# Four PSUM banks for more of the projections, four z tiles computed beside the mLSTM heads, and loads of the branch stages issued from GpSimd

## The chip, the cores and the metric

The kernel runs on one core of a Trainium2 chip. TensorE (PE) multiplies matrices into PSUM, VectorE (DVE), ScalarE (ACT) and GpSimd (POOL) work on tiles, and SyncE (SP) mostly issues transfers. Each engine runs its instructions in a fixed order that a scheduler sets when the program is built; an instruction that waits holds up everything behind it on its engine. A transfer issued by SP, ACT or POOL is one instruction in that engine's order. The metric is the time of one execution in microseconds (us), lower is better.

## What is computed

One layer of a hybrid backbone over 1024 latent tokens of width 1024, with a prefix of 256 context tokens. Two recurrent mixers read the same modulated input `u`, an mLSTM with 8 heads and a gated linear attention (GLA) with 4 heads, both in two directions. Their outputs are normalized, gated and merged, and a convolutional GLU follows. Cut to what the change touches:

```python
mod = jax.nn.silu(c) @ w_mod[l] + b_mod[l]            # 6 x 1024, the modulation vector
p = u @ w_in + b_in                                   # q, k, v, o, z and the gates of both mixers
q_m, k_m, v_m, o_m, g_m, q_g, k_g, v_g, z_g, r_g, gate_a, gate_b = jnp.split(p, cuts, axis=-1)
y_m = (head_norm(h_m, mlstm_norm_g, True) * jax.nn.sigmoid(o_m)) @ w_branch_mlstm
y_g = (head_norm(h_g, gla_norm_g, False) * jax.nn.silu(z_g)) @ w_branch_gla
mix = (jax.nn.sigmoid(gate_a) * y_m + jax.nn.sigmoid(gate_b) * y_g) @ w_out
```

## The kernel before

**Matmuls.** All float32 products are made of three matmuls in a reduced format (high x high, high x low, low x high; lines L283, L284, L285 of `mm3`), eight blocks deep: a group of 24 matmuls fills one PSUM bank of 128x512. Weights are loaded by SP in pieces, split by an ACT copy (L252) and a subtraction on DVE or POOL (L253). PSUM has eight banks in four tags of two each: `pj`, `pa`, `po`, `pt`. A group that is the third of its tag has to wait until the first one has been copied out.

**GLA stage.** For each of four heads: `gla_qk` and `gla_v` project (tag `pj`), `log_gates` (L423 to L435) makes the decays of the heads, `gla_scan` runs seven levels, each an ACT copy (L612), two PSUM tiles of products (L618, tag `pa`), and on DVE a masked copy (L619) and updates (L624, L626, L628). Level by level L618 needs the `qq` of L626. L596 is the diagonal part ahead of the levels. The scheduler places the projections of the next head and a gate tile between the levels.

**mLSTM stage.** For each of eight heads: `ml_proj_qk` of the next head (tag `pj`, with the short convolution in L727 to L747 on ACT and DVE), at every second head `ml_proj_v`, the end of the head before (`late`, L844 to L847), then `ml_scan`: POOL issues three broadcast loads per direction (L760, L762, L764), ACT takes exponentials of them in place (L765 and L769), PE multiplies (L777, L786, L796, L816, L817). Then `fill` computes gate tiles as filler: `gate_tile` makes one 128x1024 tile of the gates, two groups of tag `pj`, copied out by ACT (L537, tile `gt`) and stored to DRAM (L538) as `thb` or `tha`. Sixteen such tiles are spread over both stages.

**Branch stages.** `gated` with O_ZG computes the z tiles, takes silu of them and multiplies the GLA outputs (`hr`, loaded from DRAM). The GLA branch (L945 to L959) multiplies by its weights, 16 groups, and by the gate (`thb`, L953), and stores `ya`. In the same loop `mod_sum` forms the second part of the modulation vector, 4096 values in eight pieces: four loads of 512 KB each (L906) into two buffers in turn, eight accumulating steps on DVE (L908), after POOL has cleared the accumulator (L901) and a piece of `b_mod` has been loaded into it. `mod_row` adds the 128 partitions up with two matmuls (L913), copies the row (L914) and stores it (`md_d`, L915). There is one accumulator. SP issues all those loads and stores. Then `gated` with O_OM makes the o stage, and the mLSTM branch (L980 to L998) merges.

## Time and profile before

| | before |
|---|---|
| time, median of 3 runs | 2317.84 us (2316.33 to 2319.12) |
| the profiled execution | 2320.08 us, span 2318.3 us |
| mean granted TensorE clock | 0.991 |
| packets of transfers | 246.56 MB, mean 106 GB/s |
| stages, about | GLA 137 to 500 us, mLSTM 500 to 1100, z 1100 to 1195, GLA branch 1195 to 1285 and its row vectors to 1345, o and mLSTM branch to 1484 |

A view of waits has one row for an engine, a line and what it waited for: microseconds in total, how often, the longest. A view of windows cuts the span in stretches and gives for each engine busy time and number of instructions, the granted clock as a fraction of full speed, and the traffic. A timeline has start, duration, engine, line, output and input tiles, and in brackets the idle time before the instruction and what ended it. Times are of the profiled execution.

### The profile page before, as it was taken

How to read it: one execution, taken by the hardware profiler on the slowest of the kernel's cores; microseconds unless marked ns; L12 is line 12 of the kernel's file. 1: busy time of each engine (PE TensorE's matmuls, PEld its weight loads, DVE VectorE, ACT ScalarE, POOL GpSimd, SP SyncE). 2: the span in 40 equal slices, each digit the busy share in tenths (PEclk: the TensorE clock that was granted, in tenths of full speed). 3: DMA queues.
4: the chain of work that ended last, by engine and by line, in shares of the span. 5: the costliest groups of instructions: out<-in, count | busy, mean ns of one | idle time of the engine just before them, and what ended most of it. 6: DMA issues, size and time to landing. Idle time of an engine off the chain costs nothing.

```text
span 2318.3 us, 30341 instructions
## 1 busy us (share of the span) xinstructions
PE 2241.0 (97%) x11641; PEld 1881.1 (81%) x11641; DVE 1323.9 (57%) x2511; ACT 728.3 (31%) x1239; POOL 253.9 (11%) x254
## 2 busy tenths in 40 slices
PE   8989999998999999999999999999999999999998
PEld 4979898987888888897876788787788888888886
DVE  6485737376563665656345543477856556554257
ACT  3563323224323331322432133312433333333110
POOL 1010101011110111101110032101210000000100
PEclk9999999999999999999999999999999999999999
DMA  8231121104332433324346645524411222225721
GB/s 284 67 118 51 59 69 44 60 26 106 98 100 57 116 97 97 104 64 119 100 145 219 209 130 159 179 81 143 130 37 55 62 66 77 75 92 188 219 77 73
DMA packets 187747, 246.56 MB, mean 106 GB/s; under 512 B 16257, under 2 KB 129537, under 8 KB 187601
## 3 DMA queue, kind: packets, MB, share of 16 engines
q1 hardware_dynamic: 164673, 179.16, 24.5%
q0 software_dynamic: 12416, 44.21, 7.2%
q10 hardware_dynamic: 10512, 21.24, 2.5%
q8 instruction: 92, 1.51, 0.3%
q14 instruction: 54, 0.44, 0.1%
HBM read 186.57 MB, written 49.60 MB: 102 GB/s over the span
## 4 chain that ended last, share of the span: by engine, by line
PE 76%; DMA 8%; issue 6%; DVE 6%; ACT 2%; POOL 1%; SPq 0%; DVEq 0%; POOLq 0%; ACTq 0%
PE pj L283 15%; PE pj L284 15%; PE pj L285 15%; DMA qq<-re 2%; DMA u<-in_w_mod_dram 2%; PE pa L618 2%; PE po L284 2%; PE po L283 2%; PE po L285 2%; PE pa L285 2%; PE pa L284 2%; PE pa L283 2%; DMA s<-rr 1%; PE pt L796 1%; PE po L816 1%
## 5 line engine op out<-in xcount | busy, mean ns | idle before, releaser
L283 PE MATMUL pj<-u,whi 128*128 128x512 f32 (+1 forms) x816 | 315.8, 387 | 17.0 <-DVE s L743 5.7
L253 DVE TENSOR_TENSOR wlo<-raw,whi 128x512 fp32r<-128x512 f32 x302 | 218.0, 726 | 167.2 <-ACT whi L252 163.2
L284 PE MATMUL pj<-u,whi 128*128 128x512 f32 (+1 forms) x816 | 313.0, 384 | 0.0
L285 PE MATMUL pj<-u,wlo 128*128 128x512 f32 (+1 forms) x816 | 312.8, 384 | 0.0
L252 ACT ACTIVATE whi<-raw 128x512 fp32r<-128x512 f32 x302 | 188.8, 629 | 385.2 <-PE pj L285 155.2
L285 PE MATMUL pj<-s,wlo 128*128 128x512 f32 x784 | 305.7, 390 | 2.0 <-DVE wlo L253 2.0
L283 PE MATMUL pj<-s,whi 128*128 128x512 f32 x784 | 305.4, 390 | 0.4 <-ACT val L1118 0.4
L284 PE MATMUL pj<-s,whi 128*128 128x512 f32 x744 | 290.4, 390 | 3.0 <-POOL s L1086 3.0
L1142 DVE SCALAR_TENSOR_TENSOR acc<-g,colF,acc 128x945 f32<-128x945 f32 (+2 forms) x168 | 206.4, 1229 | 139.8 <-ACT acc L1133 137.8
L283 PEld LDWEIGHTS pj<-u,whi 128*128 128x128 f32 x816 | 155.2, 190 | 47.9 <-ACT s L769 11.1
L283 PE MATMUL pj<-whi,u 128*128 128x256 f32 x640 | 181.7, 284 | 0.0
L285 PE MATMUL pj<-whi,u 128*128 128x256 f32 x640 | 181.4, 283 | 0.0
L284 PE MATMUL pj<-wlo,u 128*128 128x256 f32 x640 | 181.4, 283 | 0.0
L285 PEld LDWEIGHTS pj<-u,wlo 128*128 128x128 f32 x816 | 155.2, 190 | 26.5
L284 PEld LDWEIGHTS pj<-u,whi 128*128 128x128 f32 x816 | 155.3, 190 | 25.7
L285 PEld LDWEIGHTS pj<-s,wlo 128*128 128x128 f32 x784 | 147.2, 188 | 33.2 <-DVE wlo L253 2.7
L283 PEld LDWEIGHTS pj<-s,whi 128*128 128x128 f32 x784 | 147.2, 188 | 32.0 <-ACT val L1118 0.8
L284 PEld LDWEIGHTS pj<-s,whi 128*128 128x128 f32 x744 | 139.7, 188 | 34.4 <-POOL s L1086 4.3
L283 PEld LDWEIGHTS pj<-whi,u 128*128 128x128 f32 x640 | 122.8, 192 | 0.5
L284 PEld LDWEIGHTS pj<-wlo,u 128*128 128x128 f32 x640 | 122.8, 192 | 0.0
L285 PEld LDWEIGHTS pj<-whi,u 128*128 128x128 f32 x640 | 122.8, 192 | 0.0
L727 DVE SCALAR_TENSOR_TENSOR s<-pj,colB,s 128x511 f32<-128x511 f32 (+2 forms) x96 | 57.5, 613 | 85.1 <-ACT s L732 84.2
(496 smaller groups left out, 4044.1 us busy)
## 6 DMA issues: line engine op xcount, KB each, us to landing
u<-in_w_mod_dram SPq DMA_DIRECT2D x48, 512.0 KB
raw<-in_w_in_dram SPq DMA_DIRECT2D x96, 256.0 KB
raw<-in_w_up_dram SPq DMA_DIRECT2D x176, 128.0 KB
raw<-in_w_in_dram SPq DMA_DIRECT2D x96, 128.0 KB
raw<-in_w_down_dram SPq DMA_DIRECT2D x44, 256.0 KB
s<-rmask POOLq DMA_DIRECT2D x16, 512.0 KB, 4.9
s<-rr POOLq DMA_DIRECT2D x16, 512.0 KB, 7.9
qq<-re POOLq DMA_DIRECT2D x16, 512.0 KB, 6.5
```

What stands on the lines that cost most here:

```text
L252: A.activation(hi, src, AF.Copy)
L253: eng.tensor_tensor(lo, src, hi.bitcast(F32), op=ALU.subtract)
L283: T.matmul(p, lh, rh, start=k == 0, stop=False)
L284: T.matmul(p, lh, rl, start=False, stop=False)
L285: T.matmul(p, ll, rh, start=False, stop=k == nk - 1)
L618: T.matmul(p[:, c, :], kc[:, o:o + P], pairs(qq, 1, hs, o, 64 // hs), start=True, stop=True)
L727: V.scalar_tensor_tensor(y[:, o:o + src.shape[1]], src, t, y[:, o:o + src.shape[1]], op0=ALU.mult, op1=ALU.add)
L796: T.matmul(p[:, i, :], kt[d][:, c, :], v[:, c, :], start=True, stop=True)
L816: T.matmul(p[:, i, :], dt_[d][:, c, :], v[:, c, :], start=True, stop=False)
L1142: V.scalar_tensor_tensor(av, g[:, r0 + dy:r1 + dy, c0 + dx:c1 + dx], convw(3 * ky + kx, f), av, op0=ALU.mult, op1=ALU.add)
```

## The change

Five edits. (1) The projections of GLA (`gla_qk`, `gla_v`, and the gate tiles beside GLA heads) take their banks from `pj` and `po` in turn instead of `pj` alone. (2) `ml_proj_qk` and the gate tiles beside mLSTM heads take theirs from `pj` and `pa` in turn; `ml_proj_v` stays with `pj`. (3) Tiles 0 to 3 of z are computed (without their tanh) as gate tiles and stored to DRAM (`thz`); the heads of the mLSTM have 2, 2, 2, 1, 1, 2, 2, 3 fills instead of 2, 2, 1, 1, 1, 1, 2, 2, and one more fill stands behind them. `gated` loads these four tiles instead of computing them. (4) In `gated`, the two branches and `mod_sum`, the loads `hr`, `thz`, `thb`, `tha`, `ya` and `w_mod` are issued by POOL instead of SP; the two `thb` loads of a tile are issued ahead of `mod_sum`. SP keeps the weights, `b_mod` and the stores. (5) The modulation sums have two accumulators (tiles 17 and 19), and the matmuls of a row come one tile later in the program.

```diff
@@ -529,10 +529,10 @@
             parts.append((hi, lo))
         return lambda k, c, n: tuple(t[:, k % 4, c:c + n] for t in parts[k // 4])
 
-    def gate_tile(dst, off, cb0, j):
+    def gate_tile(dst, off, cb0, j, tags=("pj", "pj")):
         w = wtile(w_in, off + j * P)
         for b in range(2):
-            p = proj(w, 0, b)
+            p = proj(w, 0, b, tags[b])
             t = sc.tile([P, 512], F32, tag="gt", name=nm("gt"), bufs=2)
             A.activation(t[:], p[:], AF.Identity, scale=0.5, bias=cB(cb0 + j))
             A.dma_start(dst[j][:, b * 512:b * 512 + 512], t[:])
@@ -542,10 +542,10 @@
         q = slot(0, [P, SEQ])
         k = slot(1, [P, L])
         for b in range(2):
-            p = proj(w, 0, b)
+            p = proj(w, 0, b, ("pj", "po")[b])
             A.activation(q[:, b * 512:b * 512 + 512], p[:], AF.Identity, scale=QS, bias=cB(c_qg + h))
         for b in range(3):
-            p = proj(w, P, b)
+            p = proj(w, P, b, ("pj", "po")[b % 2])
             A.activation(k[:, b * 512:b * 512 + BW[b]], p[:, 0:BW[b]], AF.Identity, bias=cB(c_kg + h))
         return q, k
 
@@ -554,7 +554,7 @@
         w = wload([(w_in, O_VG + h * 256, 256, 0)], eng=V)
         vs = [slot(2 + 2 * (h % 2) + i, [P, 5, 256]) for i in range(2)]
         for t0 in range(0, 10, 2):
-            p = pt("pj", [P, 2, 256])
+            p = pt(("pj", "po")[t0 // 2 % 2], [P, 2, 256])
             for i in range(2):
                 mm3(p[:, i, :], u_tok(t0 + i), lambda k: w(k, 0, 256))
             if t0 < 8:
@@ -728,7 +728,7 @@
                                        op0=ALU.mult, op1=ALU.add)
             for b in range(2 + i):
                 m, o = BW[b], b * 512
-                p = proj(w, i * P, b)
+                p = proj(w, i * P, b, ("pj", "pa")[(i + b) % 2])
                 A.activation(y[:, o:o + m], p[:, 0:m], AF.Identity, scale=t1, bias=bs)
                 tap(o + 1, p[:, 0:m - 1], t0)
                 tap(o, p[:, 1:m], t2)
@@ -853,11 +853,14 @@
         while rest:
             rest.pop()()
 
-    gates = [(thb_d, O_GB, c_gb, j) for j in range(8)] + [(tha_d, O_GA, c_ga, j) for j in range(8)]
-
-    def fill(n):
+    NZ = 4
+    thz_d = [drt(f"thz{j}", [P, SEQ]) for j in range(NZ)]
+    gates = [(thb_d, O_GB, c_gb, j) for j in range(8)] + [(tha_d, O_GA, c_ga, j) for j in range(8)] + \
+        [(thz_d, O_ZG, c_zg, j) for j in range(NZ)]
+
+    def fill(n, tags=("pj", "pj")):
         for _ in range(n):
-            gate_tile(*gates.pop(0))
+            gate_tile(*gates.pop(0), tags)
 
     for h in range(GH):
         q, k = gla_qk(h) if h else (q0, k0)
@@ -866,10 +869,10 @@
         if h == 0:
             for i in range(1, GH):
                 log_gates(i)
-            fill(1)
+            fill(1, ("pj", "po"))
         rest.append(gla_scan(h, q, k, v))
         if h:
-            fill(1)
+            fill(1, ("pj", "po"))
     v2 = ml_proj_v(0)
     rr_d, re_d, decb, (ta, twk, tem) = ml_gates()
     qk = ml_proj_qk(0)
@@ -881,7 +884,7 @@
         late()
         rest.append(ml_scan(h, *qk, v2[h % 2]))
         qk = nxt
-        fill(2 if h < 2 or h > 5 else 1)
+        fill((2, 2, 2, 1, 1, 2, 2, 3)[h], ("pj", "pa"))
     late()
     while gates:
         fill(1)
@@ -897,13 +900,13 @@
         return tags[seq[0] % 3]
 
     def mod_sum(b):
-        acc = ubt(19, [P, 512])
+        acc = ubt((17, 19)[b % 2], [P, 512])
         G.memset(acc[:], 0.0)
         c0 = 2048 + b * 512
         SY.dma_start(acc[0:1, :], I["b_mod"][c0:c0 + 512].unsqueeze(0))
         for k2 in range(0, KD, 2):
             raw = ubt((16, 18)[k2 // 2 % 2], [P, 2, 512])
-            SY.dma_start(raw[:], I["w_mod"][k2 * P:(k2 + 2) * P, c0:c0 + 512].rearrange("(k p) c -> p k c", p=P))
+            G.dma_start(raw[:], I["w_mod"][k2 * P:(k2 + 2) * P, c0:c0 + 512].rearrange("(k p) c -> p k c", p=P))
             for i in range(2):
                 V.scalar_tensor_tensor(acc[:], raw[:, i, :], sC[:, k2 + i, 0:1], acc[:], op0=ALU.mult, op1=ALU.add)
         return acc
@@ -917,24 +920,31 @@
     def gated(off, cb0, src_d, silu):
         hi, lo = [], []
         for j2 in range(4):
-            w = wload([(w_in, off + j2 * 256, 256, 0)])
+            pre = silu and 2 * j2 < NZ
+            w = None if pre else wload([(w_in, off + j2 * 256, 256, 0)])
             for e in range(2):
                 j = 2 * j2 + e
                 hi.append(slot(j, [P, SEQ], F32R))
                 lo.append(slot(8 + j, [P, SEQ], F32R))
                 hr = ubt(16 + j % 2, [P, SEQ])
-                SY.dma_start(hr[:], src_d[j][:])
+                G.dma_start(hr[:], src_d[j][:])
                 ht = ubt(18, [P, SEQ])
                 zz2 = ubt(19, [P, 2, 512]) if silu else None
+                if pre:
+                    G.dma_start(zz2[:].rearrange("p a b -> p (a b)"), thz_d[j][:])
                 for b in range(2):
                     s_ = slice(b * 512, b * 512 + 512)
-                    p = proj(w, e * P, b, ytag())
+                    p = None if pre else proj(w, e * P, b, ytag())
                     th = sc.tile([P, 512], F32, tag="gt", name=nm("gt"), bufs=2)
-                    A.activation(th[:], p[:], AF.Tanh, scale=0.5, bias=cB(cb0 + j))
+                    if pre:
+                        A.activation(th[:], zz2[:, b, :], AF.Tanh)
+                    else:
+                        A.activation(th[:], p[:], AF.Tanh, scale=0.5, bias=cB(cb0 + j))
                     hs = hr[:, s_]
                     if silu:
                         zt = zz2[:, b, :]
-                        A.activation(zt, p[:], AF.Identity, scale=0.5, bias=cB(cb0 + j))
+                        if not pre:
+                            A.activation(zt, p[:], AF.Identity, scale=0.5, bias=cB(cb0 + j))
                         V.tensor_tensor(hs, zt, hs, op=ALU.mult)
                     V.scalar_tensor_tensor(ht[:, s_], th[:], 1.0, hs, op0=ALU.add, op1=ALU.mult)
                     split(hi[j][:, s_], lo[j][:, s_], ht[:, s_])
@@ -942,21 +952,27 @@
 
     ya_d = [drt(f"ya{j}", [P, SEQ]) for j in range(8)]
     ghi_, glo_ = gated(O_ZG, c_zg, hg_d, True)
+    accs = {}
     for j2 in range(4):
         w = wload([(I["w_branch_gla"], j2 * 256, 256, 0)])
         for e in range(2):
             j = 2 * j2 + e
-            acc = mod_sum(j)
+            ths = []
+            for b in range(2):
+                ths.append(sc.tile([P, 512], F32, tag="gt", name=nm("gt"), bufs=2))
+                G.dma_start(ths[b][:], thb_d[j][:, b * 512:b * 512 + 512])
+            accs[j] = mod_sum(j)
             for b in range(2):
                 s_ = slice(b * 512, b * 512 + 512)
-                th = sc.tile([P, 512], F32, tag="gt", name=nm("gt"), bufs=2)
-                SY.dma_start(th[:], thb_d[j][:, s_])
+                th = ths[b]
                 A.activation(th[:], th[:], AF.Tanh)
                 p = pt(ytag(), [P, 512])
                 mm3(p[:], lambda k: w(k, e * P, P), lambda k: (ghi_[k][:, s_], glo_[k][:, s_]))
                 V.scalar_tensor_tensor(th[:], th[:], 1.0, p[:], op0=ALU.add, op1=ALU.mult)
                 SY.dma_start(ya_d[j][:, s_], th[:])
-            mod_row(j, acc)
+            if j:
+                mod_row(j - 1, accs[j - 1])
+    mod_row(7, accs[7])
 
     rowF = ubt(19, [P, 3, P])
     cw = [I["ffn_conv_w"][a, b] for a in range(3) for b in range(3)]
@@ -983,13 +999,13 @@
         for e in range(2):
             j = 2 * j2 + e
             ya = ubt(16 + j % 2, [P, SEQ])
-            SY.dma_start(ya[:], ya_d[j][:])
+            G.dma_start(ya[:], ya_d[j][:])
             xhi.append(ubt(j, [P, SEQ], F32R))
             xlo.append(ubt(8 + j, [P, SEQ], F32R))
             for b in range(2):
                 s_ = slice(b * 512, b * 512 + 512)
                 th = sc.tile([P, 512], F32, tag="gt", name=nm("gt"), bufs=2)
-                SY.dma_start(th[:], tha_d[j][:, s_])
+                G.dma_start(th[:], tha_d[j][:, s_])
                 A.activation(th[:], th[:], AF.Tanh)
                 p = pt(ytag(), [P, 512])
                 mm3(p[:], lambda k: w(k, e * P, P), lambda k: (mhi_[k][:, s_], mlo_[k][:, s_]))
```

The lines behind the change have other numbers: L906, L901, L913, L953, L958 become L909, L904, L916, L963, L972.

How the order moves, at three places. First PE between the middle levels of the scan of GLA head 0. L618 are the scan's products (`qq` against `s`), L283 to L285 the projections between them. Before, two levels have seven matmuls of 128x512 between them:

```order
L618 MATMUL pa_1447<-qq_1352,s_224_1444 128x128 x4
L618 MATMUL pa_1453<-qq_1352,s_224_1444 128x128 x4
L283 MATMUL pj_1805<-u_48_301,whi_1707 128x512
L284 MATMUL pj_1805<-u_56_309,whi_1707 128x512
L285 MATMUL pj_1805<-u_48_301,wlo_1708 128x512
L283 MATMUL pj_1805<-u_49_302,whi_1707 128x512
L284 MATMUL pj_1805<-u_57_310,whi_1707 128x512
L285 MATMUL pj_1805<-u_49_302,wlo_1708 128x512
L283 MATMUL pj_1805<-u_50_303,whi_1714 128x512
L618 MATMUL pa_1468<-qq_1352,s_227_1465 128x128 x4
L618 MATMUL pa_1474<-qq_1352,s_227_1465 128x128 x4
```

After, the two levels at the same place follow each other directly, and the fillers behind them are of 128x256:

```order
L618 MATMUL pa_1451<-qq_1356,s_224_1448 128x128 x4
L618 MATMUL pa_1457<-qq_1356,s_224_1448 128x128 x4
L618 MATMUL pa_1472<-qq_1356,s_227_1469 128x128 x4
L618 MATMUL pa_1478<-qq_1356,s_227_1469 128x128 x4
L284 MATMUL pj_1889<-wlo_1872,u_48_301 128x256
L285 MATMUL pj_1889<-whi_1871,u_56_309 128x256
L283 MATMUL pj_1889<-whi_1871,u_49_302 128x256
L284 MATMUL pj_1889<-wlo_1872,u_49_302 128x256
L285 MATMUL pj_1889<-whi_1871,u_57_310 128x256
```

Counted over all levels of this scan, from its first to its last L618, there stand 48 fillers of 128x512 and 11 of 128x256 before, and 48 of 128x256 after. For head 1 and for head 2 it is 56 of 128x512 before, 51 and one of 128x256 after; for head 3, 27 and 47 before, 3 and 91 after.

Second ACT beside mLSTM head 1, where the exponentials of the scan (L765 on `qq`, L769 on `s`) and the copies of gate tiles out of PSUM (L537) share the queue. Before:

```order
L765 ACTIVATE qq_6513<-qq_6513 128x1024
L537 ACTIVATE gt_5993<-pj_5968,colB 128x512
L769 ACTIVATE s_939_6515<-s_939_6515,ta 128x128
L538 DMA thb_873<-gt_5993 128x512
L769 ACTIVATE s_939_6515<-s_939_6515,ta 128x128 x3
L252 ACTIVATE whi_6216<-raw_6214 128x512
L769 ACTIVATE s_939_6515<-s_939_6515,ta 128x128 x4
L769 ACTIVATE s_941_6530<-s_941_6530,ta 128x128
L765 ACTIVATE qq_6513<-qq_6513 128x1024
L537 ACTIVATE gt_6021<-pj_5996,colB 128x512
```

After, the sequence is the same, and the last tile comes from a bank of `pa`:

```order
L765 ACTIVATE qq_6517<-qq_6517 128x1024
L537 ACTIVATE gt_5997<-pj_5972,colB 128x512
L769 ACTIVATE s_939_6519<-s_939_6519,ta 128x128
L538 DMA thb_873<-gt_5997 128x512
L769 ACTIVATE s_939_6519<-s_939_6519,ta 128x128 x3
L252 ACTIVATE whi_6220<-raw_6218 128x512
L769 ACTIVATE s_939_6519<-s_939_6519,ta 128x128 x4
L769 ACTIVATE s_941_6534<-s_941_6534,ta 128x128
L765 ACTIVATE qq_6517<-qq_6517 128x1024
L537 ACTIVATE gt_6025<-pa_6000,colB 128x512
```

The copies keep their places behind the exponentials; what moved is the bank from which the second one reads.

Third the GLA branch. Before, SP issues loads and stores in one row; L906 are the loads of `w_mod`, L903 of `b_mod`, L953 the gates, L958 the stores of `ya`, L915 those of a finished row:

```order
L906 DMA u_1508_10566<-in_w_mod_dram 128x2x512
L906 DMA u_1509_10570<-in_w_mod_dram 128x2x512
L953 DMA gt_10711<-thb_868 128x512
L958 DMA ya_9788<-gt_10681 128x512
L906 DMA u_1528_10665<-in_w_mod_dram 128x2x512
L906 DMA u_1529_10669<-in_w_mod_dram 128x2x512
L953 DMA gt_10764<-thb_869 128x512
L915 DMA md_d<-u_1505_10555 1x512
L958 DMA ya_9788<-gt_10711 128x512
L903 DMA u_1527_10662<-in_b_mod_dram 1x512
```

After, POOL issues the gates (L963) and `w_mod` (L909) and clears the accumulator (L904) in between:

```order
L963 DMA gt_10684<-thb_868 128x512
L909 DMA u_1537_10689<-in_w_mod_dram 128x2x512
L904 MEMSET u_1536_10686 128x512
L909 DMA u_1538_10693<-in_w_mod_dram 128x2x512
L963 DMA gt_10765<-thb_869 128x512
L909 DMA u_1539_10697<-in_w_mod_dram 128x2x512
L909 DMA u_1540_10701<-in_w_mod_dram 128x2x512
L963 DMA gt_10767<-thb_869 128x512
L909 DMA u_1547_10772<-in_w_mod_dram 128x2x512
L904 MEMSET u_1546_10769 128x512
L909 DMA u_1548_10776<-in_w_mod_dram 128x2x512
L963 DMA gt_10872<-thb_870 128x512
```

The loads of `w_mod` moved from a queue where they stood among stores of the branch to one where they stand among gate loads and the clearing of the accumulators; the stores stay on SP. On PE the matmul of a row (L916) now comes after every two groups of the branch, the first after four and the last 4 matmuls into the second group of the o stage (17 groups and 4 matmuls behind the branch's start); before, it came after every three.

## The prediction

> **What bounds the kernel now.** I read the page first, then the list of waits by engine, then windows cut at the stages, then timelines where a wait sits. The page says that TensorE (PE) carries the time.
>
> ```profile
> PE 2241.0 (97%) x11641; PEld 1881.1 (81%) x11641; DVE 1323.9 (57%) x2511; ACT 728.3 (31%) x1239; POOL 253.9 (11%) x254
> ```
>
> But 97% busy is not 97% full: a matmul's record lasts longer than the distance to the next one, so short stalls vanish in it. Counting matmuls per stretch shows them. The columns are the stretch, its length, then busy time and instructions of PE, weight loads, DVE, ACT, POOL, the granted clock, DMA share and GB/s.
>
> ```profile
> core 0: us, PE busy (x) PEld busy (x) DVE busy (x) ACT busy (x) POOL busy (x), PEclk, DMA share, GB/s
> 1682.00:1740.00 58.00, 58.00 (x258) 48.04 (x257) 31.46 (x32) 23.06 (x30) 7.18 (x3) 1.00 0.13 37
> 147.00:182.00 35.00, 32.57 (x201) 28.51 (x202) 33.08 (x55) 14.17 (x26) 9.83 (x9) 0.92 0.13 39
> 637.00:640.00 3.00, 3.00 (x9) 2.35 (x8) 1.52 (x3) 2.63 (x7) 1.12 (x1) 0.50 0.23 87
> 791.00:794.00 3.00, 2.91 (x7) 2.38 (x8) 0.08 (x2) 2.89 (x6) 1.80 (x1) 0.51 0.00 0
> 1210.00:1345.00 135.00, 126.54 (x514) 94.99 (x512) 70.31 (x102) 23.01 (x37) 3.68 (x7) 0.97 0.64 209
> ```
>
> A quiet stretch has 258 matmuls of 128x512 in 58 us: 0.225 us each. In the GLA branch stage (1210 to 1345) PE loses time to the modulation stream, in the first GLA scan (147 to 182) DVE is busy 33.08 of 35 us, and twice in the mLSTM stage the clock is halved behind a wait. The waits by name:
>
> ```profile
> PE pa L618 <- DVE qq L626: 8.3, 13, 1.6
> PE pa L596 <- DVE s L426: 4.6, 1, 4.6
> PE pt L777 <- ACT s L845: 5.6, 1, 5.6
> PE pt L913 <- DVE u L908: 4.4, 4, 1.8
> PE pt L913 <- issue: 4.1, 2, 2.2
> ```
>
> The same view for the mLSTM heads alone, 575 to 1045 us, holds nothing but waits for a pj bank:
>
> ```profile
> PE pj L283 <- DVE s L743: 5.5, 2, 2.8
> PE pj L283 <- ACT gt L537: 4.3, 2, 2.3
> PE pj L283 <- DVE s L727: 3.4, 2, 1.7
> ```
>
> **GLA stage: +8.3 us.** No row above has a GLA projection waiting for pj, so the two more banks remove nothing there. What they do is let the scheduler place projections earlier, so fewer are left as filler between the seven levels of the scan. Those levels are chained by DVE:
>
> ```profile
> 171.38 1.36 DVE L619 COPY_PREDICATED s<-lmask,pa 128x512 f32<-128x512 uint8 x2
> 172.62 1.28 DVE L626 TENSOR_TENSOR qq<-qq,s 128x512 f32<-128x512 f32 x2
> 173.94 1.29 DVE L624 TENSOR_TENSOR kk<-kk,s 128x512 f32<-128x512 f32 x2
> 176.14 0.28 PE L283 MATMUL pj<-u,whi 128*128 128x256 f32 x1
> 177.34 0.28 PE L284 MATMUL pj<-u,whi 128*128 128x256 f32 x1
> ```
>
> A level is some 4 us of DVE whatever PE does meanwhile. In the order of before, head 0 has 48 fillers of 128x512 and 11 of 128x256 between its first and last L618; a 128x256 takes 0.12 us (ten steps from 176.14 to 177.34). That is 48 x 0.225 + 11 x 0.12 = 12.1 us of cover. After, 48 of 128x256 stand there: 5.8 us, none of them at two of the levels. The 6.3 us missing are not less work; they are done elsewhere, while PE waits here. Heads 1 and 2 have 56 fillers before, 51 and one small one after: 5 x 0.225 - 0.12 = 1.0 us each. In head 3 (27 and 47, then 3 and 91) the cover stays within 0.3 us. Together 6.3 + 2.0 = 8.3 us. Lower end: the new order splits L596 by 24 matmuls, which could swallow its 4.6 us wait, and DVE has 35 - 33.08 = 1.9 us to spare: 8.3 - 4.6 - 1.9 = +1.8, so a gain is excluded by the chain. Upper end: two more half-clock stretches of 1.6 us each (next part) and 0.5 us: +12.
>
> **mLSTM heads: -16.4 us.** The reason of the bank waits stands on ACT, whose queue is in order:
>
> ```profile
> 626.39 1.06 ACT L765 ACTIVATE qq<-qq 128x1024 f32<-128x1024 f32 x1 [8.54 <-DMA qq<-re]
> 634.61 1.06 ACT L765 ACTIVATE qq<-qq 128x1024 f32<-128x1024 f32 x1 [1.72 <-DMA qq<-re]
> 635.58 0.67 ACT L537 ACTIVATE gt<-pj,colB 128x512 f32<-128x512 f32 x1
> 636.30 0.50 PE L283 MATMUL pj<-u,whi 128*128 128x512 f32 x1 [2.28 <-ACT gt L537]
> ```
>
> The copy out of the bank (L537) is queued behind an exponential that waits for the next scan's broadcast row. Two banks give at most two groups of 24 matmuls, 10.8 us, of patience; four give 21.6 us. ACT's order is the same in both programs at this place, so the copies come as late as before, but PE has two banks more. The three rows of 575 to 1045 sum to 5.5 + 4.3 + 3.4 = 13.2 us. The half-clock stretches behind two of them go too: nine matmuls in 3 us instead of 13, over 3.4 us some 7 x 0.225 = 1.6 us each, 3.2 together. Late next would be the weights' copy (L252), which is ahead of that exponential in ACT's order, and the scan's own matmuls, whose DMA inputs have landed by then. The stalls before 575 us I leave: there the second pa bank is held by a GLA head's result until its finish. So does the 5.6 us of L777, whose inputs are untouched. If PE merely runs into the next late thing, half stays: -8. If the earlier bank waits (2.7 us between 500 and 575) go as well: -19. The three more fills beside the heads and the trailing one carry the z tiles' 192 matmuls from one stage to another: nothing on PE, since both stages are PE-paced, as long as the mLSTM stage has no idle time left to fill.
>
> **z stage: 0.** Half of its tiles are now loaded. Each costs a store and a load, hidden under the 8 matmul groups of tiles 4 to 7 (8 x 5.4 = 43 us). If the cover is too short, one load stands open, at most the 7.9 us of the slowest kind on POOL's queue (row below): range -2 to +8.
>
> **GLA branch and modulation stream: -1.4 us.** Before, eight row vectors are summed on DVE from 512 KB loads, and PE turns each into a row (L913):
>
> ```profile
> 1217.45 0.52 POOL L901 MEMSET u<- 128x512 f32 x1 [16.90 <-DMA md_d<-u]
> 1222.23 0.39 PE L283 MATMUL pj<-s,whi 128*128 128x512 f32 x1
> 1227.81 0.39 PE L283 MATMUL pa<-s,whi 128*128 128x512 f32 x1
> 1229.72 1.54 DVE L908 SCALAR_TENSOR_TENSOR u<-u,sC,u 128x512 f32<-128x512 f32 x2 [0.96 <-DMA u<-in_w_mod_dram]
> 1254.75 0.99 PE pt L913 x2
> 1284.99 5.80 DMA u<-in_w_mod_dram
> 1303.56 4.74 DMA u<-in_w_mod_dram
> 1322.87 3.82 DMA u<-in_w_mod_dram
> ```
>
> A group here takes 1227.81 - 1222.23 = 5.58 us (0.2325 per matmul), a row about 0.86 more. So 1210 to 1345 holds 498 x 0.2325 + 8 x 0.86 = 122.7 us of work in 135: **12.3 us** lost. The memset row shows why one vector takes 18 to 20 us: the single accumulator waits for the store of the last one. Two accumulators remove that bubble, and PE's new order asks for a row every two groups, 2 x 5.58 + 0.86 = 12.0 us, where before it asked every three. The stream is then limited by its two load buffers: four loads in two rounds, each a load L, 1.54 us of DVE and some 0.2 us of handing over. L is the mean of the three DMA rows, 4.8 us, and the longer issue on POOL adds 0.16:
>
> ```profile
> 1606.85 0.53 POOL L1131 DMA_DIRECT2D u<-n  x1 [4.43 <-DMA y<-u]
> 1246.33 0.38 SPq L906 DMA_DIRECT2D u<-in_w_mod_dram  x1
> u<-n POOLq DMA_DIRECT2D x6, 512.0 KB, 3.9
> s<-rr POOLq DMA_DIRECT2D x16, 512.0 KB, 7.9
> 1199.26 1.29 POOL L253 TENSOR_TENSOR s<-u,s 128x512 fp32r<-128x512 f32 x1 [0.88 <-ACT s L252]
> 1201.14 0.69 DVE L957 SCALAR_TENSOR_TENSOR gt<-gt,po 128x512 f32<-128x512 f32 x1
> ```
>
> The period is p = 2 x (5.0 + 1.54 + 0.2) = 13.5 us. The stream starts when the last z split is done, 4.9 us into the first branch group (1200.55 against 1201.14 - 5.5). The eighth vector is ready at 4.9 + 8p, and PE reaches it after 17 groups, 4 matmuls and 7 rows, 94.9 + 0.9 + 6.2 = 102.0 us. Lost: 8 x 13.5 + 4.9 - 102.0 = 10.9 us instead of 12.3. Each 0.1 us of L is worth 1.6 us. The ends are L = 3.9 (p 11.3, nothing lost: -12.3) and L = 6.3, halfway from the mean to 7.9 (p 16.1, 31.7 lost: +19). I stay near the three rows of the same loads. Against quicker loads speaks the traffic: 3.67 MB per vector (weights, gates, stores) in 13.5 us is 272 GB/s, and this stretch ran at 213 with the DMA engines 65% busy:
>
> ```profile
> DMA packets 19346, 31.60 MB, mean 213 GB/s; under 512 B 1407, under 2 KB 7035, under 8 KB 19338
> q1 hardware_dynamic: 19338, 31.49, 65.3%
> ```
>
> [...]
>
> POOL's queue is in order too. Behind a load that waits for its buffer stand the next gate loads (thb); their consumers have six PSUM banks, 33 us, of patience. I cost that at nothing, and at p, that is in the upper end, if it fails.
>
> **mLSTM branch: 0.** POOL now issues three loads per tile between its splits of 1.29 us. No PE wait stands there before; range 0 to +5.
>
> Sum: +8.3 - 16.4 + 0 - 1.4 + 0 = **-9.5 us**. The profiled execution took 2320.08 us (span 2318.3 and 1.8 around it), 2.24 over the median of the runs; the difference carries over: 2317.84 - 9.5 = 2308.3 us.
>
> **Rivals.**
> - *The modulation stream becomes the bound (slower).* POOL's loads lengthen when two of them, gates and weights share the engines. It decides from L = 5.9 (p 15.3): there the sum is over +4.6 us. At L = 6.0, p is 15.5, 26.9 us are lost, the sum is +6.5: 2324 us. For it: 7.9 us on this queue in the mLSTM stage, 272 GB/s asked. Against: 7.9 is a load that accumulates; plain ones took 3.9.
> - *Each load on POOL's queue starts a little later, and no more.* L lies halfway between my 5.0 and the longest row, 5.80: 5.4, p 14.3, 17.3 us lost, sum -3.1: 2315 us, no change. For it: the longer issue (0.53 against 0.38) is the one thing on this queue that the rows show to be slower. Against: the 3.9 of its plain loads. [...]
> - *The bank waits turn into other waits.* ACT stays late, PE stops at the next thing that ACT owes: -8 in place of -16.4, sum -1.1: 2317 us. For it: nothing in ACT's order changes. Against: the six waits are all for a bank.
> - *Loads as quick as in the quiet stage.* L = 3.9, the stream keeps up with PE, sum -20.4: 2297 us. [...]
>
> **How the numbers follow.** Chances: forecast 0.39, stream bound 0.19, late start 0.11, other waits 0.15, quick loads 0.16. About 0.2%, 4.6 us, is what a measurement of this kernel can tell from no change. Faster is the forecast and quick loads, less 0.02 for the forecast's upper edge: 0.53. Same is late start, other waits and that edge: 0.28. Slower is 0.19. The forecast's own range is 2302 to 2314. The whole reaches from just below the quick loads to just above the bound stream: 2296 to 2325.
>
> **What would show it.** In the profile after: the bank waits of 575 to 1045 us gone from the list and clock 1.00 there (right); new waits of L283 on whi or of L816 on ACT (wrong). L618 waits in head 0 grown by some 6 us. L916 waits on the modulation sum: about 11 us in all, spread evenly, loads near 5 us. If loads there take over 5.9 us, the prediction fails upwards; if L618's waits do not grow, downwards.

## The result, and the profile after

The changed kernel takes 2342.76 us (median of 4 runs, 2341.47 to 2343.39) against 2317.09 us of before: ratio 1.0113, 95% interval 1.0095 to 1.0130. It is 25.7 us slower, where 9.5 us faster was forecast. The profiled execution took 2341.47 us, span 2339.5.

Both programs issue the same 11641 matmuls, in an order that differs inside a stage, so the start of the n-th one at a stage's edge, or of a named line, is the same point of the program in both. Read from the traces' matmul starts, in us:

| point of the program | before | after | change in this stretch |
|---|---|---|---|
| first L596 of GLA head 1 (head 0 done) | 232.0 | 240.0 | +8.0 |
| first L777 of mLSTM head 0 | 592.0 | 601.0 | +1.0 |
| first matmul of the GLA branch | 1195.3 | 1192.4 | -11.9 |
| 580 matmuls later (all row vectors done) | 1346.5 | 1369.9 | +26.3 |
| last matmul | 2307.9 | 2328.5 | -2.8 |

The table is of one execution each, and these are 21.4 us apart; the medians are 25.7 apart. The mLSTM heads did gain, GLA lost what was foreseen, and the GLA branch with its modulation stream lost 26 us. The list of PE's waits after says the same (line, what it waited for, microseconds in all, times, longest; rows that bear on none of these stages are left out):

```profile
PE pt L916 <- DVE u L911: 26.0, 6, 8.7
PE pa L618 <- DVE qq L626: 7.8, 12, 1.7
PE pt L777 <- ACT s L845: 6.0, 1, 6.0
PE pa L283 <- DVE s L727: 5.7, 1, 5.7
PE pa L618 <- DVE s L628: 3.7, 2, 1.9
PE pt L916 <- issue: 2.7, 1, 2.7
PE pa L596 <- DVE s L426: 2.6, 1, 2.6
```

The two rows of L916, 28.7 us, answer to the 8.5 us of L913 before. The windows of the mLSTM heads and of the GLA branch after:

```profile
core 0: us, PE busy (x) PEld busy (x) DVE busy (x) ACT busy (x) POOL busy (x), PEclk, DMA share, GB/s
575.00:1045.00 470.00, 469.73 (x2903) 418.46 (x2902) 270.04 (x797) 147.43 (x291) 59.10 (x56) 1.00 0.35 97
1192.00:1370.00 178.00, 149.32 (x584) 110.97 (x583) 83.37 (x123) 32.89 (x57) 48.28 (x68) 0.92 0.61 190
```

Beside the heads PE has no idle time left and the full clock (before, 456.63 of 470 us at 0.99). In the branch it is idle 28.7 of 178 us, and the granted clock is 0.92: behind some of the longer waits it falls (0.60 from 1246 to 1254 us, at a wait of 6.0 that ends at 1248.2), which costs time on top: there matmuls start 0.43 us apart from 1250.59 to 1252.30 and 0.23 apart from 1252.55 on.

Where the 26 us come from stands in the chain of waits of this stage. One piece a row: start, length, what it was (the shortest pieces are left out). Two turns of it:

```profile
1248.06 0.69 DVE gt L971
1248.77 6.32 DMA ya<-gt
1255.13 0.49 issue
1255.64 0.53 POOL gt L963
1256.20 6.12 DMA u<-in_w_mod_dram
1262.41 0.76 DVE u L911
1263.19 0.75 DVE u L911
1264.38 0.76 DVE u L911
1265.34 0.49 issue
1265.83 0.69 DVE gt L971
1266.54 5.42 DMA ya<-gt
1272.00 0.49 issue
1272.51 0.57 POOL gt L963
1273.08 0.59 issue
1273.71 0.67 POOL u L909
1274.38 6.32 DMA u<-in_w_mod_dram
```

It is a loop. A w_mod load lands, DVE adds it up (L911) and then takes a finished group out of PSUM (L971), which stood behind; SP stores that group (ya); only when the store has landed is the gate buffer free for the next gate load (L963), which stands on POOL's queue ahead of the next w_mod load. From 1248.06 to 1265.83 one turn takes 17.8 us, and the eight row vectors come 16.7 us apart on average (1214.8 to 1331.9, seven steps). The forecast took 13.5. Not every turn is like this: from 1230 to 1340 us the chain passes through a store of ya four times (20.8% of it) and through w_mod loads for 46.5%, and from 1280 to 1307 it is loads and sums alone. POOL's own waits in this stage name the same release:

```profile
POOL gt L963 <- DMA ya<-gt: 56.3, 11, 6.5
POOL u L909 <- DVE u L911: 19.1, 16, 4.7
```

### The profile page after: what moved, and what is told of

The parts are those of the page before. It is cut to its first block, busy times and chain, and to the rows that moved or that the text cites. A ratio compares the mean times of both kernels' runs of the same rounds, so it can differ in the third digit from the quotient of the medians.

```text
span 2339.5 us, 30400 instructions
## 1 busy us (share of the span) xinstructions
PE 2246.9 (96%) x11641; PEld 1887.1 (81%) x11641; DVE 1323.6 (57%) x2511; ACT 728.8 (31%) x1239; POOL 309.5 (13%) x346
## 4 chain that ended last, share of the span: by engine, by line
PE 78%; DMA 9%; DVE 6%; issue 5%; ACT 2%; POOL 1%; SPq 0%; DVEq 0%; POOLq 0%; ACTq 0%
PE pj L285 13%; PE pj L283 13%; PE pj L284 13%; DMA u<-in_w_mod_dram 4%; PE pa L283 3%; PE pa L284 3%; PE pa L285 3%; PE po L285 2%; PE po L283 2%; PE po L284 2%; PE pa L618 2%; DMA ya<-gt 1%; PE po L816 1%; PE pt L796 1%; PE po L817 1%
## 5 line engine op out<-in xcount | busy, mean ns | idle before, releaser
L285 PE MATMUL pj<-s,wlo 128*128 128x512 f32 x792 | 309.3, 391 | 0.5 <-DVE wlo L253 0.4
L283 PE MATMUL pj<-s,whi 128*128 128x512 f32 x792 | 309.4, 391 | 0.4 <-ACT val L1134 0.4
L1158 DVE SCALAR_TENSOR_TENSOR acc<-g,colF,acc 128x945 f32<-128x945 f32 (+2 forms) x168 | 204.9, 1220 | 139.1 <-ACT acc L1149 137.0
L283 PE MATMUL pj<-u,whi 128*128 128x512 f32 (+1 forms) x456 | 178.4, 391 | 0.0
L284 PE MATMUL pj<-u,whi 128*128 128x512 f32 (+1 forms) x456 | 177.6, 389 | 0.0
L285 PE MATMUL pj<-u,wlo 128*128 128x512 f32 (+1 forms) x456 | 177.0, 388 | 0.0
L283 PEld LDWEIGHTS pj<-s,whi 128*128 128x128 f32 x792 | 149.1, 188 | 33.9 <-ACT gt L968 1.1
L285 PEld LDWEIGHTS pj<-s,wlo 128*128 128x128 f32 x792 | 149.0, 188 | 32.6 <-DVE wlo L253 1.4
L283 PE MATMUL pa<-u,whi 128*128 128x512 f32 (+1 forms) x384 | 145.0, 378 | 5.7 <-DVE s L727 5.7
L284 PE MATMUL pj<-wlo,u 128*128 128x256 f32 x512 | 145.4, 284 | 0.3 <-DVE wlo L253 0.3
L285 PE MATMUL pj<-whi,u 128*128 128x256 f32 x512 | 144.9, 283 | 0.0
L283 PE MATMUL pj<-whi,u 128*128 128x256 f32 x512 | 144.9, 283 | 0.0
L284 PE MATMUL pa<-u,whi 128*128 128x512 f32 (+1 forms) x384 | 144.6, 377 | 0.0
L285 PE MATMUL pa<-u,wlo 128*128 128x512 f32 (+1 forms) x384 | 143.9, 375 | 0.0
L283 PEld LDWEIGHTS pj<-u,whi 128*128 128x128 f32 x456 | 86.7, 190 | 15.8 <-ACT s L392 0.7
L284 PEld LDWEIGHTS pj<-u,whi 128*128 128x128 f32 x456 | 86.7, 190 | 15.2
L285 PEld LDWEIGHTS pj<-u,wlo 128*128 128x128 f32 x456 | 86.5, 190 | 15.2
L284 PEld LDWEIGHTS pj<-wlo,u 128*128 128x128 f32 x512 | 98.2, 192 | 0.6 <-DVE wlo L253 0.5
```

The source lines that it names most:

```text
L283: T.matmul(p, lh, rh, start=k == 0, stop=False)
L284: T.matmul(p, lh, rl, start=False, stop=False)
L285: T.matmul(p, ll, rh, start=False, stop=k == nk - 1)
L1158: V.scalar_tensor_tensor(av, g[:, r0 + dy:r1 + dy, c0 + dx:c1 + dx], convw(3 * ky + kx, f), av, op0=ALU.mult, op1=ALU.add)
```

## The experiments

Times are medians. Kernels were measured in four groups, each with its own runs of the kernel before (2317.07, 2319.3, 2319.17 and 2318.41 us), so the ratio to those is given too, and a difference between groups is uncertain by some 2 us. "Branch" is the time of the 580 matmuls from the first of the GLA branch on, from the profile of one execution: 151.2 us before, 177.5 after. Four kernels of the first table have the same code in the branch (the changed one and those without the GLA banks, the mLSTM banks and the z tiles); there it took 172.4 to 177.5 us, so a difference of 3 us in this column says little.

| kernel | us | ratio to before (95%) | branch, us |
|---|---|---|---|
| changed kernel | 2342.8 | 1.0113 (1.0095 to 1.0130) | 177.5 |
| gate loads on SP | 2329.3 | 1.0045 (1.0031 to 1.0059) | 165.3 |
| w_mod loads on SP | 2322.7 | 1.0026 (1.0013 to 1.0038) | 162.2 |
| both on SP | 2314.6 | 0.9988 (0.9969 to 1.0006) | 151.5 |
| four gate buffers, all on POOL | 2328.2 | 1.0047 (1.0033 to 1.0062) | 164.6 |
| GLA projections in pj alone | 2328.8 | 1.0042 (1.0019 to 1.0064) | 174.5 |
| mLSTM projections in pj alone | 2355.0 | 1.0154 (1.0131 to 1.0177) | 172.4 |
| no z tiles among the fills | 2333.7 | 1.0063 (1.0040 to 1.0085) | 174.9 |
| kernel before + mLSTM banks alone | 2296.7 | 0.9911 (0.9893 to 0.9930) | 152.8 |

**What slows the row vectors.** First the gate loads were taken off POOL's queue, then the w_mod loads, then both.

```diff
-                G.dma_start(ths[b][:], thb_d[j][:, b * 512:b * 512 + 512])
+                SY.dma_start(ths[b][:], thb_d[j][:, b * 512:b * 512 + 512])
```

> The changed kernel with the gate loads (thb) of the GLA branch back on SP's queue; the loads of w_mod stay on POOL's. In the changed kernel the eight row vectors of the modulation follow each other at 16.7 us, and PE loses about 39 us from the first group of the GLA branch to the row vectors' end (13 before). Theory queue: a w_mod load stands on POOL behind a gate load, which waits for the store of ya that frees its buffer, so each vector runs once round load, DVE sum, copy out of PSUM, store, gate load; without the gates in that queue the period falls to 2 x (L + 1.74) with L near 5, some 13.5 us, and the time falls by 20 to 28 us. Theory buffers: two load buffers and loads of 6.0 us set 15.5 us anyway; the time falls by 0 to 10 us.

```diff
-            G.dma_start(raw[:], I["w_mod"][k2 * P:(k2 + 2) * P, c0:c0 + 512]...
+            SY.dma_start(raw[:], I["w_mod"][k2 * P:(k2 + 2) * P, c0:c0 + 512]...
```

> The changed kernel with the w_mod loads back on SP's queue; the gate loads stay on POOL's. Theory queue: the chain is cut here as well, period near 13.5 us, the time falls by 20 to 28 us. Theory buffers: loads on POOL's queue are longer by themselves (6.0 against 4.8 us); on SP's the period is 2 x (4.8 + 1.74) = 13.1 us, the time falls by 20 to 28 us here but by at most 10 with only the gates moved.

Both edits together:

> The changed kernel with gate loads and w_mod loads both back on SP's queue, with the stores of ya among them, and two accumulators. Theory queue: what counts is that gate loads that wait stand ahead of w_mod loads, on whichever queue; the period stays at 15 us or more and the time falls by less than 12 us. Theory buffers: SP's loads are short, the period is 13.1 us, the time falls by 20 to 28 us.

Neither theory holds alone. With the gates on SP the time fell by 13.5 us, less than the queue theory's 20 to 28 and more than the 10 of the buffers; with w_mod on SP by 20.0; with both by 28.2, and the branch is back at 151.5 us. The queue theory's forecast for this last one (a period of 15 us or more) is refuted: on SP gate and w_mod loads stand in one queue as well, and the vectors come 13.6 us apart; the gate loads wait 16.1 us there for the stores of ya, not 56.3. With w_mod alone on SP they come 14.7 us apart, and stores of ya are still 16.8% of the chain (1220 to 1320 us): the two edits are not independent. Taken in this order w_mod is worth 15.3 us of branch and the gates 10.7; in the other, 12.2 for the gates and 13.8 for w_mod.

In the kernel with the gates on SP, what POOL waits for in the stage is now mostly the load buffers, and of the stores only that of a finished row (md_d), no longer that of ya:

```profile
POOL u L909 <- DVE u L911: 69.6, 26, 6.2
POOL u L909 <- DMA md_d<-u: 7.9, 2, 4.2
```

and its chain in this stretch is loads and sums alone, each load followed by its two steps of DVE:

```profile
1288.35 6.05 DMA u<-in_w_mod_dram
1294.50 0.76 DVE u L911
1295.28 0.76 DVE u L911
1296.05 0.29 issue
1296.34 4.84 DMA u<-in_w_mod_dram
1301.27 0.76 DVE u L911
1302.06 0.76 DVE u L911
1303.11 4.80 DMA u<-in_w_mod_dram
```

Its vectors are 14.9 us apart. Between this kernel and the one with both on SP only the issuer of the w_mod loads differs, and that is 14.7 us of time and 13.8 us of branch. A row of each timeline shows a part of it, the issue of one such load, first with the loads on POOL, then on SP:

```profile
1286.43 0.72 POOL L909 DMA_DIRECT2D u<-in_w_mod_dram  x1 [6.22 <-DVE u L911]
```

```profile
1243.98 0.37 SPq L909 DMA_DIRECT2D u<-in_w_mod_dram  x1
```

How long a load is on its way is recorded for POOL's queue alone (median 5.2 us here, from issue to landing). On SP the chain of waits has a part of them: 15 loads stand singly in it from 1190 to 1345 us, 3.0 to 7.6 us, median 4.9. Two loads one behind the other in each vector make 2 x 0.3 = 0.6 us of the 1.3 by which the period fell, as an estimate. A second thing moved with the loads: on POOL the store of a row (md_d) is named in front of w_mod loads, 7.9 us in all, and on SP's queue in front of none. What each is worth was not separated.

**Is it the wait for the store, or the traffic on that queue?** Here the gate loads stay on POOL, in the same places, and get two buffers more, for which the two accumulators share a tile.

```diff
+    accp = ubt(19, [P, 2, 512])
+    thq = ubt(17, [P, 2, 512])
-        acc = ubt((17, 19)[b % 2], [P, 512])
+        acc = accp[:, b % 2, :]
-                ths.append(sc.tile([P, 512], F32, tag="gt", name=nm("gt"), bufs=2))
+                ths.append(thq[:, b, :] if j % 2 else sc.tile([P, 512], F32, tag="gt", ..., bufs=2)[:])
```

> The changed kernel with the gate loads still on POOL's queue, in the same places among the w_mod loads, but with four gate buffers instead of two (two of them in the halves of tiles that the accumulators left free), so that a gate load waits for the store of ya of two tiles before and not of one. Nothing else is moved. Theory queue: what made the vectors slow is that wait, ahead of the w_mod loads; the period falls from 16.7 to at most 15 us and the time by at least 10 us, about as far as with the gates moved to SP (-13.5). Theory transfers: POOL's queue is slower because it carries more bytes, whatever waits on it; the period stays above 16 us and the time within 5 us of the changed kernel.

-14.5 us, as much as taking the gates off the queue. The vectors come 15.1 us apart, a hair over the 15 expected. The theory of transfers, with over 16 us and a time within 5, is refuted. POOL's waits for the stores of ya, now from two kinds of buffer, are 11.3 + 13.9 us where they were 56.3:

```profile
POOL u L909 <- DVE u L911: 36.5, 20, 3.3
POOL u L965 <- DMA ya<-u: 13.9, 5, 4.9
POOL gt L965 <- DMA ya<-gt: 11.3, 4, 4.3
```

and the median landing of a w_mod load is 5.0 us here against 6.0. So the wait on the queue is shown as the cause of about half of the 26 us, 12.2 to 12.9 of branch. The other half, 13.8, goes when SP issues the w_mod loads; of what on POOL's side it consists stays open.

**The GLA projections.**

```diff
-            p = proj(w, 0, b, ("pj", "po")[b])
+            p = proj(w, 0, b)
-            p = proj(w, P, b, ("pj", "po")[b % 2])
+            p = proj(w, P, b)
-            p = pt(("pj", "po")[t0 // 2 % 2], [P, 2, 256])
+            p = pt("pj", [P, 2, 256])
-            fill(1, ("pj", "po"))
+            fill(1)
```

> The changed kernel with the GLA projections and the gate tiles beside GLA heads back in pj alone, so that 48 fillers of 128x512 stand between the levels of head 0's scan again, where the changed kernel has 48 of 128x256. Theory fillers: the stage of head 0 is 8 us shorter again (the L596 of head 1 comes at 232 and not at 240 us), the time falls by 7 to 9 us. Rival: the 8 us come from the place of L596 and the decays ahead of the scan and not from the fillers; then more than half of them are lost ahead of the first L618, and this kernel shows that.

-14.0 us, more than expected. Head 1's L596 comes at 230.5 instead of 240.0, which is 9.5. The place is inside and behind the scan, not ahead of it: the first L618 comes at 147.7 here, 147.2 in the changed kernel and 149.4 before, and from there to the L596 of head 1 it is 82.8, 92.8 and 82.6 us. The rival, the place of L596, is out. In the changed kernel PE has less to do beside the first levels, 25.30 us of 35 where it was 32.57, while DVE goes on much as before (31.20 where it was 33.08); that fits the fillers, which were not changed by themselves:

```profile
147.00:182.00 35.00, 25.30 (x185) 23.82 (x184) 31.20 (x50) 11.48 (x22) 10.18 (x9) 0.95 0.08 23
```

In the profiles 1.5 us more are saved up to the first mLSTM head, where the changed kernel waits 5.7 us for a `pa` bank (L283 for L727, in the list above) and this one 1.9, and 1.1 beside the heads. The branch is 3.0 shorter, no more than it varies without an edit to it.

**The banks of the mLSTM stage, and the z tiles.** First each was undone in the changed kernel.

```diff
-                p = proj(w, i * P, b, ("pj", "pa")[(i + b) % 2])
+                p = proj(w, i * P, b)
-        fill((2, 2, 2, 1, 1, 2, 2, 3)[h], ("pj", "pa"))
+        fill((2, 2, 2, 1, 1, 2, 2, 3)[h])
```

> The changed kernel with the mLSTM projections and the gate tiles beside the mLSTM heads back in pj alone. Theory banks: the waits for a pj bank and their half-clock stretches come back, the first group of the GLA branch moves from 1192 to 1205 to 1210 us, the time rises by 13 to 18 us. Rival: with the new GLA stage ahead and three more fills the waits fall elsewhere; the time rises by less than 8 us.

+12.2 us (two runs), a little under the 13 to 18 expected; the first group of the branch moves from 1192.4 to 1207.9, 15.5 us, as expected. Then the banks were put into the kernel before, alone, with its own fills.

```diff
-                p = proj(w, i * P, b)
+                p = proj(w, i * P, b, ("pj", "pa")[(i + b) % 2])
-        fill(2 if h < 2 or h > 5 else 1)
+        fill(2 if h < 2 or h > 5 else 1, ("pj", "pa"))
```

> The kernel before with one edit alone: the mLSTM projections and the gate tiles beside the mLSTM heads take pj and pa in turn. Theory of the prediction: the bank waits between 575 and 1045 us and the half-clock stretches behind two of them go, 16.4 us, so 2301 to 2305 us. Rival: the waits return at the next thing that ACT owes; half of it, 8 us, or less. Taking the same banks away from the changed kernel cost 12 us.

2296.7 us, 0.7 to 1.1% faster than before and 4 us under the lower end expected. In the profiled executions the difference is 16.4 us (spans 2318.3 and 2301.9), in the medians 21.7; the profiled one was the slowest of four. Between 575 and 1045 us its list of PE's waits is empty, and the window reads:

```profile
575.00:1045.00 470.00, 469.61 (x2937) 419.11 (x2936) 279.04 (x858) 142.26 (x288) 64.92 (x61) 1.00 0.36 98
```

The z tiles:

```diff
-    NZ = 4
+    NZ = 0
-        fill((2, 2, 2, 1, 1, 2, 2, 3)[h], ("pj", "pa"))
+        fill((2, 2, 1, 1, 1, 1, 2, 2)[h], ("pj", "pa"))
```

> The changed kernel with all eight z tiles computed in the z stage again and the fills of before (2, 2, 1, 1, 1, 1, 2, 2, none behind). Theory neutral: the 192 matmuls only move, the first group of the GLA branch comes within 3 us of 1192, the time is within 3 us. Rival: as fillers they covered waits of the mLSTM heads, or their loads delay the z stage; then the branch's start moves by 5 us or more, one way or the other.

-9.0 us in the medians (two runs) and 5.8 in the spans, of which 2.2 come before the branch. The neutral theory's time (within 3 us) is refuted for the changed kernel; its other sign, a start of the branch within 3 us, held, and the 5 us of its rival did not show. Ahead of the branch PE waits 1.83 us for weights that DVE split late, a wait that the kernel without these tiles lacks:

```profile
1173.43 0.50 PE L285 MATMUL po<-u,wlo 128*128 128x512 f32 x1 [1.83 <-DVE wlo L253]
```

**Towards a faster kernel.** The parts that lost were taken out together: the GLA projections in `pj` alone, gate and w_mod loads on SP, by the diffs above.

> The changed kernel without its edit to the GLA projections (banks of pj alone there) and with gate and w_mod loads on SP's queue again; the banks of the mLSTM stage, the z tiles and the two accumulators stay. If the parts add: 2314.6 (both loads on SP) less the 12 to 14 us that the GLA projections cost, 2301 to 2303 us, faster than the kernel before by 0.6 to 0.7%. If they share a cause: 2310 or more.

2301.0 us, ratio 0.9926 (0.9909 to 0.9942), as expected if the parts add. From there three more edits, alone and together. A third load buffer, in the tile that the second accumulator leaves when both share one:

```diff
-            raw = ubt((16, 18)[k2 // 2 % 2], [P, 2, 512])
+            raw = ubt((16, 18, 17)[(4 * b + k2 // 2) % 3], [P, 2, 512])
```

> The faster version (no change to the GLA projections, gate and w_mod loads on SP, two accumulators) with a third buffer for the w_mod loads, in the tile that the second accumulator gave up (both accumulators now share one tile). There the row vectors still come 13.2 us apart, where PE asks for one every 12.0, and PE waits 8.2 us for them. Theory buffers: the two load buffers set what is left; with three the period is PE's own 12.0 us, PE's waits for the vectors fall under 3 us, and the time falls by 4 to 7 us (2294 to 2297). Rival, transfers: with 3.67 MB per vector the transfer engines themselves are the limit; the third buffer lengthens each load, and the time stays within 2 us of 2301.

No z tiles among the fills, and then both:

> The faster version with all z tiles computed in the z stage and the fills of before. In the changed kernel that took 9.1 us off the median and 5.8 off the profiled span, 2.2 of it before the GLA branch, where PE waited for weights split late by DVE. Theory: the four loaded z tiles bring DVE, ACT and POOL more work in the z stage than its eight matmul groups cover, here too; the time falls by 3 to 9 us. Rival: most of it was the loads on POOL's queue of the changed kernel, which this version does not have; the time falls by less than 3 us.

> Third load buffer and no z tiles among the fills, together. If both theories hold, 7 to 13 us under the faster version, 2288 to 2294 us. If neither, within 3 us of 2301.

The loads of the change that were still on POOL:

```diff
-                G.dma_start(hr[:], src_d[j][:])
+                SY.dma_start(hr[:], src_d[j][:])
-                    G.dma_start(zz2[:].rearrange("p a b -> p (a b)"), thz_d[j][:])
+                    SY.dma_start(zz2[:].rearrange("p a b -> p (a b)"), thz_d[j][:])
-            G.dma_start(ya[:], ya_d[j][:])
+            SY.dma_start(ya[:], ya_d[j][:])
-                G.dma_start(th[:], tha_d[j][:, s_])
+                SY.dma_start(th[:], tha_d[j][:, s_])
```

> The faster version with the remaining loads that the change gave to POOL (hr, thz, ya, tha) back on SP's queue. Theory: they cost and bring nothing, as no PE wait stands behind them; the time stays within 2 us. Rival: a queue of their own is worth something in the o stage and the mLSTM branch, or costs there; 4 us or more, one way or the other.

The same without z tiles, with the third buffer, and with both:

> The version with all loads on SP and unchanged GLA projections (2292.7 us), with all z tiles in the z stage. Theory: the z tiles cost only through their loads and the splits on POOL's queue, so without loads on POOL they cost nothing; the time stays within 2 us. Rival: they cost by the work of loading and storing them; 3 to 5 us less, as with the loads on POOL.

> The version with all loads on SP and unchanged GLA projections (2292.7 us), with the third load buffer for w_mod. If what was left of PE's waits for the row vectors (6.1 us) is the buffers' alone: 2286 to 2289 us. If not: 2291 or more.

> As the one with the third buffer, and all z tiles in the z stage. By the theory on the z tiles the same time as with them, within 2 us.

What was measured, from the version as it is to all three edits:

| version (all: GLA in pj alone, mLSTM banks, two accumulators, gates and w_mod on SP) | us | ratio to before (95%) | branch, us |
|---|---|---|---|
| as it is | 2301.0 | 0.9926 (0.9909 to 0.9942) | 150.3 |
| third load buffer | 2298.8 | 0.9905 (0.9885 to 0.9926) | 146.8 |
| no z tiles among the fills | 2297.9 | 0.9903 (0.9883 to 0.9923) | 150.2 |
| both of these | 2293.2 | 0.9886 (0.9863 to 0.9909) | 142.6 |
| remaining loads on SP | 2292.7 | 0.9882 (0.9857 to 0.9907) | 147.2 |
| remaining loads on SP, no z tiles | 2296.1 | 0.9905 (0.9890 to 0.9919) | 147.9 |
| remaining loads on SP, third buffer | 2290.8 | 0.9886 (0.9871 to 0.9901) | 141.6 |
| all three | 2286.1 | 0.9864 (0.9848 to 0.9881) | 143.4 |

The third buffer does what the theory of buffers says: the vectors come 12.3 us apart, PE's own pace, and its waits for them (8.2 us) are down to 0.5. But PE now waits for weight copies there instead, which it did not before:

```profile
PE pa L283 <- ACT whi L252: 4.5, 3, 3.0
```

The gain in the time, 2.2 us alone, is under the 4 to 7 expected, and the intervals overlap; in the spans it does not show (2298.1 and 2298.2), though the branch is 3.5 us shorter, since the stages ahead ran 3.7 us longer in that execution. Moving the remaining loads off POOL gained 8.4 us, where nothing was expected: that theory is refuted. In the profiles 1.8 of it come before the branch, where the wait for late weights (1.6 us) is gone, 3.1 in the branch and 1.7 behind it. The z tiles stay open where POOL issues no loads: taking them out cost 3.4 us in one pair and gained 4.7 in the other, with intervals that overlap in both; neither is within the 2 us that the theory on their loads expected. Both edits together gave 7.9 us (7 to 13 expected), and the third buffer without loads on POOL gave 1.9 (2290.8, between the 2289 of its theory and the 2291 of its rival).

The last version, 2286.1 us, is the fastest of all, 1.4% under the kernel before. In its stage from 1170 to 1370 us, PE waits for one thing only, a weight copy:

```profile
PE pj L283 <- ACT whi L252: 2.5, 1, 2.5
```

## Why the prediction was wrong, point by point

- **GLA, +8.3:** the mechanism fits and the size is near, in part by luck. The first head lost 8.0 us (forecast 6.3), but these are 10.2 from the first L618 on less 2.2 that the scan began earlier, and L618's waits of all kinds grew from 10.7 to 16.5 us in the list, 5.8 against "some 6". Heads 1 and 2 lost nothing (106.6 to 106.9 us each in both programs, forecast 1.0 each). All in all, undoing it gave 14 us: what it does behind the scans, at the `pa` bank that waits for L727 among others, was not in the term.
- **mLSTM heads, -16.4:** right in mechanism and sign, and about in size. The banks alone give 16.4 us in the profiled executions and 21.7 in the medians; that the first is the same figure is luck. The ledger's -11.9 holds the z stage too: without the z tiles among the fills that stretch is 3.2 us shorter. The rival that the waits only move is out: no wait is left there. In the profile of before the clock was halved behind a wait of 2.28 us that ends at 636.30. The 3.4 us of half clock in the forecast's sum are near what that profile has: granted clocks of 0.97 from 636 to 637 us, 0.50 from 637 to 640 and 0.64 from 640 to 640.5 make 0.06 + 3.0 + 0.36 = 3.4 us at half, as an estimate, and matmuls start 0.42 us apart from 637.2 to 640.2.
- **GLA branch and modulation stream, -1.4: this step failed.** It came out as +26.3. The form of the sum holds: with the measured 16.7 us for p, 8p + 4.9 - 102.0 = 36.5 us lost, 24.2 more than the 12.3 before. With both loads on SP, where p is 13.6, it gives 11.7 us lost, about the 12.3 of before, and the branch took 0.3 us more than before: what is left of the change in the branch, the two accumulators above all, brought nothing there. (A slip in it, seven rows at 0.86 us put at 6.2 instead of 6.0, moves it by 0.2.) What failed is p, 13.5 us, for two reasons. First the sentence that "behind a load that waits for its buffer stand the next gate loads", costed at nothing because the gates' consumers had patience. It looked at the queue from one side: behind a gate load that waits for its buffer stand the next w_mod loads, which have no patience at all. The order in the section on the change shows it, gate and w_mod loads in turn on POOL. Four buffers for the gates took POOL's waits for those stores from 56.3 to 25.2 us and gave 14.5 us. Second, what a load costs when POOL issues it: 5.0 us were taken from SP's rows with 0.16 for the issue. With POOL as issuer the issue is 0.72 against 0.37, the median landing 6.0, and without the gates' wait still 5.2, with a period of 14.9. The sum with 5.2 gives 2 x (5.2 + 1.54 + 0.2) = 13.9; the other 1.0 us per vector is in the 0.2 of handing over, and what fills it is open. That "plain ones took 3.9" was read from a quiet stage alone: beside the mLSTM heads (575 to 700 us, before) loads on this queue that do not accumulate (they spread a row or a mask over partitions) had taken longer, and with them p would have been 14.1 to 15.9:

```profile
s<-rmask POOLq DMA_DIRECT2D x4, 512.0 KB, 5.3
qq<-re POOLq DMA_DIRECT2D x4, 512.0 KB, 6.2
```

- **z stage and mLSTM branch, 0:** too low where it could be measured. In the faster version all loads that remained on POOL cost 8.4 us, in its profiles 1.8 ahead of the branch and 1.7 behind it; the upper ends of these terms (+8 and +5) hold that. In the changed kernel it was not measured by itself.
- **Rivals:** the bound modulation stream, given 0.19, was nearest to the case that came. Its point of decision, L = 5.9, was passed by a hair (6.0), and its 2324 us were short by 19, for the loop and for what the GLA and z terms lacked.

## What to carry to other kernels

When a load moves to another engine's queue, write down for each load in that queue what it waits for, and ask of each what stands behind it, in both directions: a load with patience ahead of one without makes the second wait for the first one's buffer (here 56.3 us of POOL's waits, of which four buffers left 25.2). Give extra PSUM banks to the stage whose waits name a bank and to no other: beside the mLSTM heads they gave 21.7 us (2318.41 to 2296.7); in the GLA stage, where no projection waited for one, they only changed the order, and fillers that covered a chain on DVE were gone from it; undoing that gave 14.0 us.

## What was not expected of the hardware

The same 512 KB load took 0.72 us to issue on POOL and 0.37 on SP, and with the gate loads on SP 14 us of a stage of 150 hung on which of the two issued 32 of them. The chip's transfer engines were not the limit: with the loads on SP the stage moved 222 GB/s and took 151.5 us, on POOL 190 GB/s and 177.5. Issuing gate and w_mod loads from POOL beside SP gained the kernel nothing: with both kinds on SP it was 28.2 us faster. The longer issue alone is 32 x 0.35 = 11.2 us of POOL, less than the 13.8 us lost, and part of it lies beside loads on their way (with the gates on SP, POOL issues one at 1286.43 and the next at 1288.35 us, and the median landing is 5.2); what makes up the rest was not separated.
